# Attention on one core: a head's last two key and value pieces are split in its own first slots, and the last head's weight copies begin later

## The chip, the cores and the metric

The kernel runs on one core of one Trainium2 chip. The core has a matrix engine (PE, with its weight loads shown apart as PEld), three elementwise engines (DVE, ACT, POOL) and a queue for transfers (SP), each with an instruction stream of its own that runs in order; they meet through semaphores. The metric is the device time of one execution in microseconds (us); a kernel's time is the median of its timed runs.

## The reference, cut to what matters

One decoder block on a sequence of 2048 positions, model width 1024, eight attention heads of width 128, all in 32-bit floats. The part that the change touches is the attention:

```python
s = jnp.einsum('bhqd,bhkd->bhqk', qi, k, preferred_element_type=jnp.float32) * scale
s = s + (ci[:, :, :, None] - c[:, :, None, :])            # forget gates: c is a running sum
s = jnp.where(kpos[None, :] <= qpos[:, None], s, -jnp.inf) # causal
w = jax.nn.softmax(s, axis=-1)
return jnp.einsum('bhqk,bhkd->bhqd', w.astype(v.dtype), v)
```

Before it stand a norm, the input projection and a recurrent branch; after it the output projection `w_out`, another norm and a gated embedding. The last head's part of the attention overlaps with the preparation of `w_out`.

## The kernel before, in words

**Split operands.** Every matrix product is made of three: each 32-bit operand is split into a high part (a rounded copy) and a low part (the rest), and `mm3` (lines 63 to 70) multiplies high by high, high by low and low by high. So each operand must be split before PE can read it. `split` (line 52) makes the high part on ACT (line 54) and the low part on DVE or POOL (line 60).

**Slots.** The attention runs over 8 heads, each cut into four units g = 0 to 3 of 512 query positions; unit g sees 4(g+1) key blocks of 128. A unit's key blocks each take one slot, so a head takes 4 + 8 + 12 + 16 = 40 slots, and `t0` holds the slot in which each unit begins. In this text a *place* is a slot counted from the first slot of its head (0 to 39), and heads are counted from 0. In one slot `run_slot` writes, in this order: what is listed in `before` for that slot (mostly transfers on SP); the scores of a later unit (`score_units`: PE fills a bank `sbank`, line 1298 on DVE adds the bias, writes `pr` and takes the row's minimum `m`, line 1307 on ACT takes the exponential); the value product of three slots ago (`add_values`, PE into `obank`); the turning of this slot's probabilities (`turn_probs`: PE transposes into `tbank`, line 1342; ACT makes `th`, line 54; DVE makes `tl`, line 60); a finished unit's gate (`gate_unit`, DVE, line 1370); and then what is listed in `after` (splits, masks, chores). This is the order of each engine's own instructions and nothing else: an engine that is ahead of the others runs on until a semaphore stops it, and SP is commonly some slots ahead.

**Bringing a head in.** While head h-1 runs, the keys and values of head h are loaded in eight pieces of 128x512, p = 0 to 7: even pieces are keys (512 positions each), odd ones values. `load_piece` (lines 1184 and 1186) issues the transfer into the tile `kvf`, of which there are three; `split_piece` makes `kh` or `vh` on ACT and `kl` or `vl` on POOL. A piece's buffer is free again when POOL has made the low part, so a load can be stopped on SP by the split of the piece three before it. The tiles of two successive heads lie in two pools (`kvA`, `kvB`).

**What else uses the same engines.** Each unit's queries are loaded (`qf`, line 1216) and split into `qh` on ACT (line 1235) and `ql` on DVE (line 1237). Each unit loads a row `bias` (line 1222) and four rows `dg` (line 1228), and POOL adds the causal mask to `dg` (line 1153). A finished unit's squares go to POOL (lines 1379 and 1380) and its result is stored (line 1387). In heads 0 to 6, 64 chores are laid out one every four slots, at the places 2, 6, 10 and so on: each loads something, makes one POOL operation (`scale_l`, line 1479, or `make_t`, line 1496) and stores it (lines 1482 and 1499).

**The last head** (7) brings no further head in. Instead `load_w` (line 1253), `w_high` (ACT, line 1256) and `w_low` (POOL, line 1260) copy and split the first weights of the output projection, in the tile `wst` with three buffers, eight copies into `wa` and three into `wb`; `first_low` (DVE, line 1574) splits the first of its operands at place 16. The copies read no attention data. `open_w1` gives the weights the space of pool `kvA`, which head 6 used.

The loads and splits of a head are placed by

```python
for p_ in range(8):
    a = base + (13, 16, 26, 28, 31, 33, 36, 38)[p_]
    at(before, a - 4, lambda h=h, p_=p_: load_piece(h, p_))
    at(after, a, lambda h=h, p_=p_: split_piece(h, p_))
```

where `base` is the first slot of head h-1. Within one slot the lists keep the order in which they were filled: units' loads first, then pieces, weights, chores.

Of the kernel before, what the change touches and what calls it, by code (L numbers as in the profile page):

```python
# [20 lines left out]
KD = D // P  # L21
# [26 lines left out]
def f32(ap):  # L48
    return ap.bitcast(F32)


def split(nc, src, hi, lo, eh, el):
    if eh == "act":
        nc.scalar.activation(hi, src, AF.Copy)  # L54
    elif eh == "dve":
        nc.vector.tensor_copy(hi, src)
    else:
        nc.gpsimd.tensor_copy(hi, src)
    eng = nc.vector if el == "dve" else nc.gpsimd
    eng.tensor_tensor(out=lo, in0=src, in1=f32(hi), op=ALU.subtract)  # L60
# [13 lines left out]
def hymba_kernel(ctx: ExitStack, tc: tile.TileContext, x, xT, pT, w_p, w_v, w_o, w_ple, w_pg,  # L74
                 w_gates, vecs, rows, mgrp, out):
    nc = tc.nc
# [869 lines left out]
    for i in range(8):  # L946
        h, c = jobs.pop(0)
# [30 lines left out]
    for i in range(24):  # L978
        h, c = jobs.pop(0)
# [200 lines left out]
    def load_piece(h, n):  # L1180
        c = n // 2
        f = ap.tile([P, 4, P], F32, name="kvf", bufs=3)
        if n % 2 == 0:
            nc.sync.dma_start(out=f.rearrange("p a b -> p (a b)"), in_=kT_d[h, :, c * 512:(c + 1) * 512])
        else:
            nc.sync.dma_start(out=f, in_=v_d[h, :, c * 4:c * 4 + 4])
        pieces[h, n] = f

    def split_piece(h, n):
        if n == 0:  # L1190
            s = Ctx()
            kv = kvB if h % 2 else kvA
            s.kh = kv.tile([P, S], F32R, name="kh")
            s.kl = kv.tile([P, S], F32R, name="kl")
            s.vh, s.vl = {}, {}
            heads[h] = s
        s = heads[h]
        f = pieces.pop((h, n))
        c = n // 2
        if n % 2 == 0:  # L1200
            cs = slice(c * 512, (c + 1) * 512)
            split(nc, f.rearrange("p a b -> p (a b)"), s.kh[:, cs], s.kl[:, cs], "act", "pool")
        else:
            bs, a = slice(c % 2 * 4, c % 2 * 4 + 4), c // 2
            if c % 2 == 0:
                kv = kvB if h % 2 else kvA
                s.vh[a] = kv.tile([P, 8, P], F32R, name=f"vh{a}")
                s.vl[a] = kv.tile([P, 8, P], F32R, name=f"vl{a}")
            split(nc, f, s.vh[a][:, bs], s.vl[a][:, bs], "act", "pool")
# [41 lines left out]
    def load_w(n, k):  # L1251
        w_raw[n, k] = w1s[0].tile([P, 512], F32, name="wst", bufs=3)
        nc.sync.dma_start(out=w_raw[n, k], in_=W_SOURCE[W_ORDER[n]](k))

    def w_high(n, k):
        nc.scalar.activation(WO[n % 2][k][:, :512], w_raw[n, k], AF.Copy)

    def w_low(n, k, eng):
        w = WO[n % 2][k]
        eng.tensor_tensor(out=w[:, 512:], in0=w_raw.pop((n, k)), in1=f32(w[:, :512]), op=ALU.subtract)  # L1260
# [136 lines left out]
    before = {}  # L1397
    after = {}

    def at(d, slot, f):  # L1400
        d.setdefault(max(slot, 0), []).append(f)
# [36 lines left out]
        at(after, a, lambda p_=p_: split_piece(0, p_))  # L1438
    for h in range(1, NH):
        base = t0[4 * (h - 1)]  # L1440
        for p_ in range(8):
            a = base + (13, 16, 26, 28, 31, 33, 36, 38)[p_]
            at(before, a - 4, lambda h=h, p_=p_: load_piece(h, p_))
            at(after, a, lambda h=h, p_=p_: split_piece(h, p_))

    def open_w1():
        kvA_stack.close()
# [5 lines left out]
    w1s = []  # L1453
    last0 = t0[4 * (NH - 1)] + AHEAD + 1
    at(before, last0, open_w1)
    for a, (n, k) in zip((0, 2, 3, 5, 6, 8, 9, 11, 23, 26, 29), [(0, k) for k in range(KD)] + [(1, k) for k in range(3)]):
        a += last0
        at(before, a, lambda n=n, k=k: load_w(n, k))
        at(after, a + 4, lambda n=n, k=k: w_high(n, k))
        at(after, a + 4, lambda n=n, k=k: w_low(n, k, nc.gpsimd))  # L1460

    def scales_rows():
        b = psT.tile([P, 512], F32, name="tbank")
# [553 lines left out]
```

## Time and profile before

| | |
|---|---|
| time, median of 3 runs | 2072.45 us (2070.7 to 2072.69) |
| the profiled execution, its own time | 2074.98 us |
| its span, first to last instruction | 2073.2 us |
| granted TensorE clock | 1.000 |
| busy: PE / PEld / DVE / ACT / POOL | 2057.1 / 1742.4 / 1621.7 / 1151.5 / 697.0 us |
| first and last `th` of the attention (ACT, line 54) | 1046.7 and 1587.8 us into the span |
| key and value pieces loaded within it | 58 |

Busy time is the share in which an engine had work; on PE, matmuls overlap, so a busy PE may still be held up for less than a matmul's length. An idle time in square brackets stands in the row of the instruction that ended it, with what released that instruction. The rows themselves are shown with the prediction.

### The profile page before, as it was taken

The page shows a single profiled execution, that of the slowest core. Times are in us where ns is not written, and L with a number is a line of the kernel's source. Part 1 is how long each engine was busy: PE and PEld are TensorE (multiplying, and loading weights), DVE is VectorE, ACT ScalarE, POOL GpSimd, SP SyncE. Part 2 cuts the span into 40 slices and gives each one's busy share as a digit, 9 for nine tenths or more (in the row PEclk, how much of TensorE's full clock was granted, in tenths as well). Part 3 has the DMA queues.
Part 4 walks back from the last instruction along what each step waited for, and adds up shares of the span by engine and source line. Part 5 has one row for each costly group of instructions (what it writes and reads, how often), then busy time and mean ns, then how long its engine had stood idle before and what let it go on. Part 6 is the DMA issues. An engine that isn't in the chain of part 4 may idle for free.

```text
span 2073.2 us, 31244 instructions
## 1 busy us (share of the span) xinstructions
PE 2057.1 (99%) x10599; PEld 1742.4 (84%) x10599; DVE 1621.7 (78%) x2689; ACT 1151.5 (56%) x1855; POOL 697.0 (34%) x612
## 2 busy tenths in 40 slices
PE   9999999999999999999999999999999999999999
PEld 6988888888988898888888878888888888888887
DVE  8977997696749877986388878888885778776676
ACT  7536665344237776874167767777774344442232
POOL 4333555333013335633135665666642000000000
PEclk9999999999999999999999999999999999999999
DMA  9698898987899888779867767778653887665553
GB/s 346 215 324 296 318 348 307 375 315 282 270 283 277 276 272 293 253 258 324 253 191 236 247 209 216 237 234 241 195 173 124 291 244 231 190 216 181 171 177 117
DMA packets 254675, 518.63 MB, mean 250 GB/s; under 512 B 24866, under 2 KB 91698, under 8 KB 254515
## 3 DMA queue, kind: packets, MB, share of 16 engines
q1 hardware_dynamic: 254368, 516.59, 75.7%
q8 instruction: 83, 1.36, 0.3%
q14 instruction: 78, 0.63, 0.1%
q10 hardware_dynamic: 146, 0.05, 0.0%
HBM read 314.29 MB, written 202.25 MB: 249 GB/s over the span
## 4 chain that ended last, share of the span: by engine, by line
PE 93%; DVE 4%; DMA 1%; issue 1%; ACT 1%; POOL 0%; SPq 0%; DVEq 0%; POOLq 0%; ACTq 0%
PE bank L68 15%; PE bank L70 15%; PE bank L69 15%; PE pbank L70 7%; PE pbank L68 7%; PE pbank L69 7%; PE tbank L1342 5%; PE sbank L68 4%; PE sbank L70 3%; PE sbank L69 3%; PE obank L69 3%; PE obank L70 3%; PE obank L68 3%; PE bank L1884 1%; PE tbank L1361 1%
## 5 line engine op out<-in xcount | busy, mean ns | idle before, releaser
L68 PE MATMUL bank<-XH,op 128*128 128x512 f32 x876 | 342.8, 391 | 0.9 <-DVE u L375 0.9
L70 PE MATMUL bank<-XH,op 128*128 128x512 f32 x876 | 341.4, 390 | 0.0
L69 PE MATMUL bank<-XL,op 128*128 128x512 f32 x876 | 341.4, 390 | 0.0
L375 DVE TENSOR_TENSOR c<-bank,c 128x512 f32<-128x512 f32 x280 | 186.3, 684 | 109.5 <-PE bank L70 103.0
L60 DVE TENSOR_TENSOR tl<-tbank,th 128x512 fp32r<-128x512 f32 (+1 forms) x320 | 192.0, 606 | 78.7 <-ACT th L54 77.0
L54 ACT ACTIVATE th<-tbank 128x512 fp32r<-128x512 f32 (+1 forms) x320 | 167.4, 530 | 108.7 <-PE tbank L1342 102.3
L68 PEld LDWEIGHTS bank<-XH,op 128*128 128x128 f32 x876 | 164.6, 188 | 35.1 <-ACT op L297 1.1
L69 PEld LDWEIGHTS bank<-XL,op 128*128 128x128 f32 x876 | 164.6, 188 | 34.4 <-issue 0.5
L70 PEld LDWEIGHTS bank<-XH,op 128*128 128x128 f32 x876 | 164.5, 188 | 34.2
L1307 ACT ACTIVATE pr<-pr,m 128x1024 f32<-128x1024 f32 (+14 forms) x128 | 150.3, 1175 | 36.1 <-DVE m L1298 35.3
L1342 PE MATMUL tbank<-ident,pr 128*128 128x128 f32 x1062 | 167.4, 273 | 0.0
L152 POOL TENSOR_TENSOR rsm<-rs,mhalf 128x1 f32<-128x1 f32 x16 | 8.7, 541 | 435.0 <-DVE rs L151 435.0
L1342 PEld LDWEIGHTS tbank<-ident,pr 128*128 128x128 f32 x1062 | 130.5, 140 | 27.5 <-DVE tl L60 0.3
L68 PE MATMUL sbank<-kh,qh 128*128 128x512 f32 (+3 forms) x320 | 135.3, 423 | 3.5 <-DVE m L1298 3.0
L68 PE MATMUL obank<-th,vh 128*128 128x512 f32 (+1 forms) x320 | 123.4, 386 | 1.8 <-ACT th L54 1.8
L297 ACT ACTIVATE op<-wq 128x512 fp32r<-128x512 f32 (+1 forms) x95 | 59.5, 629 | 111.1 <-PE bank L70 82.4
L69 PE MATMUL obank<-tl,vh 128*128 128x512 f32 (+1 forms) x320 | 117.9, 369 | 0.2 <-DVE tl L60 0.2
L70 PE MATMUL obank<-th,vl 128*128 128x512 f32 (+1 forms) x320 | 116.9, 365 | 0.0
L70 PE MATMUL sbank<-kh,ql 128*128 128x512 f32 (+3 forms) x320 | 115.9, 362 | 0.0
L69 PE MATMUL sbank<-kl,qh 128*128 128x512 f32 (+3 forms) x320 | 115.3, 360 | 0.0
L69 PE MATMUL bank<-XL,wr 128*128 128x512 f32 x244 | 95.1, 390 | 0.0
L68 PE MATMUL bank<-XH,wr 128*128 128x512 f32 x244 | 95.1, 390 | 0.0
(359 smaller groups left out, 5763.8 us busy)
## 6 DMA issues: line engine op xcount, KB each, us to landing
wo_d<-op SPq DMA_DIRECT2D x140, 512.0 KB, 5.3
op<-wo_d SPq DMA_DIRECT2D x79, 512.0 KB, 6.0
wr<-wo_d SPq DMA_DIRECT2D x61, 512.0 KB, 6.2
wq<-in_w_p_dram SPq DMA_DIRECT2D x40, 512.0 KB, 6.1
wst<-wt_d SPq DMA_DIRECT2D x56, 256.0 KB, 3.5
vo_d<-op SPq DMA_DIRECT2D x27, 516.0 KB, 4.3
wst<-in_w_o_dram SPq DMA_DIRECT2D x40, 256.0 KB, 3.2
X<-xr_d SPq DMA_DIRECT2D x32, 257.5 KB, 4.0
```

Source lines behind the costliest of these rows:

```text
L54: nc.scalar.activation(hi, src, AF.Copy)
L60: eng.tensor_tensor(out=lo, in0=src, in1=f32(hi), op=ALU.subtract)
L68: nc.tensor.matmul(out, lhsT=wh, rhs=xh, start=start, stop=False)
L69: nc.tensor.matmul(out, lhsT=wh, rhs=xl, start=False, stop=False)
L70: nc.tensor.matmul(out, lhsT=wl, rhs=xh, start=False, stop=stop)
L152: nc.gpsimd.tensor_tensor(out=o, in0=t, in1=mhalf[:, :n], op=ALU.pow)
L297: nc.scalar.activation(op[:, :n], self.source(i, hf), AF.Copy)
L375: nc.vector.tensor_tensor(out=o, in0=x, in1=y, op=ALU.add)
L1307: nc.scalar.activation(pr[0][:, a:z], pr[0][:, a:z], AF.Exp, bias=m2, scale=-1.0, accum_out=u.rs[:, c:c + 1])
L1342: nc.tensor.transpose(b[:, i * P:(i + 1) * P], u.P[i][:, sb * P:(sb + 1) * P], ident)
L1361: nc.tensor.transpose(b[:, i * P:(i + 1) * P], u.r4[:, i:i + 1].broadcast_to([P, P]), ident)
L1884: nc.tensor.transpose(b[:, k * P:(k + 1) * P], u.xt[:, kk * P:(kk + 1) * P], ident)
```

## The change

Two lists of slots are changed, and nothing in what is computed.

For each head h from 1 on, the split of piece 6 (the last 512 keys) moves from place 36 of head h-1 to place 6 of head h, and that of piece 7 (the last 512 values) from place 38 to place 10. Pieces 0 to 5 are split where they were. Each load is placed 7 slots ahead of its split instead of 4, but not before the slot after the split of the piece that had the same buffer: pieces 0 to 5 at the places 6, 9, 19, 21, 24, 27 (before: 9, 12, 22, 24, 27, 29), and pieces 6 and 7 at place 39 of head h-1 and place 3 of head h (before: 32 and 34). In SP's order piece 5's load thereby comes ahead of the `bias` and `dg` loads of place 29, which it followed before.

In the last head the eight copies into `wa` are made at the places 12, 13, 14, 16, 17, 18, 20, 21 (before: 8, 10, 11, 13, 14, 16, 17, 19), and the three into `wb` stay at 31, 34, 37. Their loads are issued 3 slots ahead instead of 4.

```diff
     for h in range(1, NH):
         base = t0[4 * (h - 1)]
-        for p_ in range(8):
-            a = base + (13, 16, 26, 28, 31, 33, 36, 38)[p_]
-            at(before, a - 4, lambda h=h, p_=p_: load_piece(h, p_))
-            at(after, a, lambda h=h, p_=p_: split_piece(h, p_))
+        places_ = (13, 16, 26, 28, 31, 33, 46, 50)
+        for p_, a in enumerate(places_):
+            at(before, base + max(a - 7, places_[p_ - 3] + 1 if p_ > 2 else 0), lambda h=h, p_=p_: load_piece(h, p_))
+            at(after, base + a, lambda h=h, p_=p_: split_piece(h, p_))
...
-    for a, (n, k) in zip((0, 2, 3, 5, 6, 8, 9, 11, 23, 26, 29), [(0, k) for k in range(KD)] + [(1, k) for k in range(3)]):
+    for a, (n, k) in zip((8, 9, 10, 12, 13, 14, 16, 17, 27, 30, 33), [(0, k) for k in range(KD)] + [(1, k) for k in range(3)]):
         a += last0
-        at(before, a, lambda n=n, k=k: load_w(n, k))
-        at(after, a + 4, lambda n=n, k=k: w_high(n, k))
-        at(after, a + 4, lambda n=n, k=k: w_low(n, k, nc.gpsimd))
+        at(before, a - 3, lambda n=n, k=k: load_w(n, k))
+        at(after, a, lambda n=n, k=k: w_high(n, k))
+        at(after, a, lambda n=n, k=k: w_low(n, k, nc.gpsimd))
```

## The prediction

> **What bounds the kernel now.** I read the page first: the span, PE's busy time and the engines of the chain of work that ended last.
>
> ```profile
> span 2073.2 us, 31244 instructions
> PE 2057.1 (99%) x10599; PEld 1742.4 (84%) x10599; DVE 1621.7 (78%) x2689; ACT 1151.5 (56%) x1855; POOL 697.0 (34%) x612
> PE 93%; DVE 4%; DMA 1%; issue 1%; ACT 1%; POOL 0%; SPq 0%; DVEq 0%; POOLq 0%; ACTq 0%
> ```
>
> PE sets the time, and it idles 2073.2 - 2057.1 = 16.1 us in all. A change that takes no work from PE can win only idle time, and this one only what lies in the attention. So I next cut the attention at the starts of the heads (shown: heads 1, 2, 3, 4 and 6); columns length, then busy time (and count) of PE, PEld, DVE, ACT, POOL.
>
> ```profile
> 1112.60:1178.50 65.90, 65.43 (x393) 56.27 (x392) 56.43 (x138) 47.94 (x90) 39.29 (x42) 1.00 0.77 242
> 1178.50:1247.40 68.90, 66.05 (x394) 56.29 (x393) 56.09 (x138) 48.00 (x90) 40.75 (x43) 1.00 0.71 216
> 1247.40:1313.30 65.90, 65.41 (x393) 56.28 (x392) 56.64 (x138) 48.07 (x90) 40.09 (x43) 1.00 0.76 225
> 1313.30:1379.00 65.70, 65.21 (x393) 56.37 (x392) 56.19 (x138) 47.97 (x90) 40.51 (x43) 1.00 0.70 224
> 1445.40:1510.70 65.30, 65.21 (x394) 56.20 (x393) 55.63 (x138) 48.16 (x91) 37.88 (x42) 1.00 0.69 206
> ```
>
> Two things are to be had. Head 2 (second row) is 68.90 - 65.90 = 3.0 us longer than its neighbours. And heads 1, 3 and 4 are 0.4 to 0.6 us longer than head 6 (65.90, 65.90 and 65.70 against 65.30), with PE idle 65.90 - 65.43 = 0.47 against 0.09. Third view: who held PE up within the attention (total, times, longest).
>
> ```profile
> PE sbank L68 <- DVE m L1298: 3.0, 6, 0.8
> PE obank L68 <- ACT th L54: 1.8, 1, 1.8
> ```
>
> Fourth: the timeline at these two places. In head 2, the load of piece 5 on SP, then ACT, then PE:
>
> ```profile
> 1225.46 1.66 SPq L1186 DMA_DIRECT2D kvf<-v_d  x1
> ...
> 1236.75 0.63 ACT L54 ACTIVATE vh<-kvf 128x512 fp32r<-128x512 f32 x1 [3.45 <-DMA kvf<-v_d]
> 1237.91 0.50 PE L68 MATMUL obank<-th,vh 128*128 128x512 f32 x1 [1.81 <-ACT th L54]
> ```
>
> ACT stood 3.45 us before piece 5's split because its load had not landed, and the `th` behind it in ACT's order came late. In head 3, place 37, with head 6 below it:
>
> ```profile
> 1305.54 1.29 POOL L1496 TENSOR_TENSOR qh<-qh,qh 128x512 f32<-128x512 f32 x1
> 1306.80 1.28 POOL L60 TENSOR_TENSOR kl<-kvf,kh 128x512 fp32r<-128x512 f32 x1
> 1307.18 1.45 DVE L1237 SCALAR_TENSOR_TENSOR ql<-qf,qh 128x512 fp32r<-128x512 f32 x1
> 1309.29 0.44 PE L68 MATMUL sbank<-kh,qh 128*128 128x384 f32 x1 [0.49 <-DVE m L1298]
> ...
> 1504.11 1.29 POOL L60 TENSOR_TENSOR kl<-kvf,kh 128x512 fp32r<-128x512 f32 x1 [1.69 <-ACT kh L54]
> 1505.31 0.68 DVE L1237 SCALAR_TENSOR_TENSOR ql<-qf,qh 128x512 fp32r<-128x512 f32 x1
> ```
>
> In head 3 `ql` starts while POOL makes piece 6's `kl` and takes 1.45 us; in head 6, with `kl` nearly done, 0.68. It ends about as long after `kl` as a free `ql` lasts, so DVE waits out the POOL instruction. The 0.77 us are lost by PE, whose next bank waits for the minimum behind `ql`.
>
> **Part one: head 2's late piece.** Piece 5 comes ahead of `bias` and `dg` in SP's order, so these five transfers no longer stand before it. The load itself is not issued sooner: it waits for its buffer, that of piece 2, whose `kl` ends at 1293.10 + 1.29 = 1294.39 in head 3, and it is issued at 1294.41:
>
> ```profile
> 1287.62 0.38 SPq L1222 DMA_DIRECT2D bias<-nb_d  x1
> 1288.05 2.63 SPq L1228 DMA_DIRECT2D dg<-nb_d  x4
> 1294.41 0.32 SPq L1186 DMA_DIRECT2D kvf<-v_d  x1
> 1295.33 0.61 SPq L1216 DMA_DIRECT2D qf<-qT_d  x1
> ...
> 1293.10 1.29 POOL L60 TENSOR_TENSOR kl<-kvf,kh 128x512 fp32r<-128x512 f32 x1 [6.72 <-ACT kh L54]
> ...
> DMA to landing us min/median/max: 3.3/5.1/11.2
> ```
>
> The last row is for all loads of `kvf`. Head 2's piece 5 is issued at 1225.46 and lets ACT start at 1236.75, the maximum of 11.2; at the median it would land at 1230.6, well before ACT asks for it (1236.75 - 3.45 = 1233.3). So in the profiled execution -3.0 us, with ends 0 and -3.0. The timed runs need not have this wait: the profiled execution took 2074.98 us, 2.53 more than the median of 2072.45, and one wait for a transfer is just of that size. I count half of it against the median, -1.5.
>
> **Part two: piece 6 leaves place 36.** If POOL were then free, `ql` would take 0.68 and 0.6 us would come back in each of heads 1 to 5: -3.0 us. But POOL runs on to its next instruction, which is the chore of place 38. In head 3 that is
>
> ```profile
> 1312.90 1.29 POOL L1479 TENSOR_TENSOR kvs<-kvs,pr 128x512 f32<-128x512 f32 x1
> ...
> 1298.64 1.01 SPq L1476 DMA_DIRECT2D kvs<-yl_d  x1
> ```
>
> whose input was requested at 1298.64; all loads of `kvs` land 6.1 us later at the median, so near 1304.7, before POOL ends the chore of place 34 at 1305.54 + 1.29 = 1306.83. The chore takes the place of `kl`, lasts as long (1.29 against 1.28), and `ql` waits again. Ends -3.0 and 0; I take one head in five, -0.6, since in heads 1 and 5 this chore must wait for four transfers at once. The Trainium skill (SBUF — State Buffer, Who interferes with whom) says the same of any such pair: a DVE instruction with two SBUF inputs and a GpSimd one that reads SBUF exclude each other, and the later waits in full. The rows above agree (1.45 against 0.68); by that rule alone the sum would have 0 here instead of -0.6.
>
> **Part three: the new places 6 and 10.** Two ACT copies of 0.62 and two POOL operations of 1.29 us a head arrive there. Head 4 shows the cover:
>
> ```profile
> 1326.49 0.60 ACT L54 ACTIVATE th<-tbank 128x512 fp32r<-128x512 f32 x1 [0.43 <-PE tbank L1342]
> 1333.26 0.28 ACT L54 ACTIVATE th<-tbank 128x128 fp32r<-128x128 f32 x1 [0.71 <-PE tbank L1342]
> ...
> 1327.97 0.69 DVE L60 TENSOR_TENSOR tl<-tbank,th 128x512 fp32r<-128x512 f32 x1
> 1325.58 0.95 DVE L1370 TENSOR_TENSOR gs<-on,gs 128x512 f32<-128x512 f32 x1
> 1325.94 1.75 POOL L1479 TENSOR_TENSOR kvs<-kvs,pr 128x512 f32<-128x512 f32 x1
> ```
>
> ACT idles 0.43 us after place 6 and 0.71 after place 10, against 0.62 for a copy. The 0.2 us left over at place 7 fall on a `th` that is ready at 1326.49 + 0.60 = 1327.09 and that DVE takes up at 1327.97. DVE's only SBUF-to-SBUF operation there, `gs` at place 6, is made before ACT ends that place, so the new `kl` comes after it. I take 0; without that cover each would cost what `ql` does, 0.6 in seven heads, +4.2.
>
> **Part four: what piece 5 now holds up.** SP stops at piece 5 until POOL frees the buffer, as before, but `bias` and four `dg` now stand behind it:
>
> ```profile
> SPq L1186 <- POOL kl L60: 27.0, 13, 3.7
> ...
> 1305.50 0.55 DVE L1298 CUSTOM_DVE_ANT_0 pr<-sbank,bias 128x384 f32<-128x384 f32 x1
> 1304.76 0.62 ACT L1235 ACTIVATE qh<-qf 128x512 fp32r<-128x512 f32 x1
> ...
> DMA to landing us min/median/max: 4.4/7.5/10.4
> ...
> DMA to landing us min/median/max: 3.7/6.0/9.9
> ```
>
> The last two rows are for `dg` and for `qf`. In head 3 five transfers move from 1287.62 to 1294.8, and `qf` behind them from 1295.33 by 0.38 + 2.63 = 3.0 us to 1298.3. At its median landing it is there at 1304.3, 0.4 us before ACT reads it at 1304.76; at the longest, 1308.2, ACT waits 3.5 us, and head 2 shows the price, 3.0 us of span for 3.45 of ACT. `bias`, issued at 1294.8, is read at 1305.50, 10.7 us later; the `dg`, issued up to 1297.8, land by 1305.3 at the median, are masked by POOL and read after it, the widest last. Ends 0 and +3.0 in each of heads 1 to 6, +18; I take +1.0 in all, nearer to the median landing. Piece 6 and 7 themselves have room: their loads come after SP's stop.
>
> **Part five: the last head.** Eight copies of the same length at other places. One stays at place 16, where it meets `first_low`:
>
> ```profile
> 1541.57 1.29 POOL L1260 TENSOR_TENSOR wa<-wst,wa 128x512 fp32r<-128x512 f32 x1 [1.33 <-ACT wa L1256]
> 1541.62 2.33 DVE L1574 TENSOR_TENSOR xl<-yf,xh 128x1024 fp32r<-128x1024 f32 x1
> L1617 DVE TENSOR_TENSOR xl<-yf,xh 128x1024 fp32r<-128x1024 f32 x6 | 7.3, 1219 | 0.3 <-ACT xh L1614 0.3
> ```
>
> 2.33 against 1.22 us free, as now: 0, with ends -1.1 (the meeting ends) and +1.1 (another of that kind). The first products read `wa` at place 22, after the last copy at 21, and want only its first two tiles.
>
> **The sum.** Against the profiled execution: -3.0 - 0.6 + 0 + 1.0 + 0 = -2.6, so 2074.98 becomes 2072.4. Against the median, with half of head 2's wait: -1.5 - 0.6 + 1.0 = -1.1, so 2072.45 becomes **2071.3**.
>
> **Rivals.** (a) All idle time goes: the chore is not ready in time at any head and head 2's wait was in the timed runs too: 2072.45 - 3.0 - 3.0 = 2066.4. For it: head 6, with no chore there, has the free `ql`. Against it: the request at 1298.64. (b) Slower: `qf` is late at place 36 in heads 1 to 6, because transfers that ran while SP stood now start when it goes on. Each us that ACT waits costs 3.0/3.45 = 0.87; it decides from about 1.1 us a head, where 6 x 0.95 = 5.6 exceeds what head 2 gives by 4.1: 2076.6; at 1.5 us it is 2072.45 - 1.5 + 7.8 = 2078.8. For it: 0.4 us of room at the median. Against it: two transfers of pieces 6 and 7 leave the same stretch, and `kh` leaves ACT just after `qh`. (c) The change doesn't load sooner: piece 5 is issued at the same instant, head 2's wait stays and `ql` still waits: 2072.45.
>
> **How the numbers follow.** Single measurements of this kernel cannot tell less than 0.2%, 4.1 us, from no change: faster means under 2068.3, slower over 2076.6. The forecast with its neighbourhood has 0.50, (c) 0.14, (a) 0.19, (b) 0.17. So faster 0.19, same 0.64, slower 0.17. The range reaches to (a) below and to where (b) begins to decide above: 2066.4 to 2076.6.
>
> **What would show it.** Part one: head 2 as long as its neighbours and no ACT row that waits for `kvf`. Part two: at place 37 POOL shows L1479 or L1496 where `kl` stood, and `ql` still lasts 1.4 us in heads 3 and 4; if it lasts 0.68, (a) holds. Part three: `ql` and `gs` no longer than before at the places 6 to 15. Part four: `bias` and `dg` issued behind piece 5 and the idle time of `qh` (line 1235) before `qf`, now nearly nothing; over 1 us a head is (b). Part five: `xl` at 2.33. An idle PE behind a split at place 6 or 10 would make all of it wrong.

## The result, and the profile after

The changed kernel takes 2093.76 us, the median of 4 runs (2089.99 to 2096.68), against 2072.23 us for the kernel before on the same chip: a ratio of 1.0101, 95% interval 1.0089 to 1.0113. It is 1% slower, where 2071.3 us and "no change" were forecast, and it lies far outside the range, which ended at 2076.6. Of the rivals, (b) came true, but it had been priced at 2076.6 to 2078.8 us.

The profiled execution of the changed kernel took 2094.18 us. From its page, the span and the busy times:

```profile
span 2092.4 us, 31255 instructions
PE 2064.1 (99%) x10599; PEld 1748.4 (84%) x10599; DVE 1620.9 (77%) x2689; ACT 1150.0 (55%) x1855; POOL 700.3 (33%) x612
```

The span is 2092.4 - 2073.2 = 19.2 us longer, and two things make it up. PE idles 2092.4 - 2064.1 = 28.3 us instead of 16.1: 12.2 more. And the same 10599 matmuls keep PE busy for 2064.1 us instead of 2057.1: 7.0 more. Cut by heads (heads 0, 2, 3 and 4; columns as before the change, the third from the end is the granted clock):

```profile
1045.90:1117.20 71.30, 67.16 (x387) 56.55 (x387) 56.42 (x139) 47.73 (x93) 31.87 (x37) 0.98 0.63 190
1186.20:1255.30 69.10, 66.50 (x394) 57.40 (x393) 55.87 (x137) 47.79 (x90) 41.09 (x43) 0.98 0.72 215
1255.30:1321.60 66.30, 65.20 (x394) 56.26 (x392) 55.36 (x136) 47.82 (x90) 40.11 (x41) 1.00 0.74 219
1321.60:1394.20 72.60, 67.42 (x394) 57.42 (x393) 57.63 (x139) 47.77 (x91) 41.40 (x45) 0.98 0.73 212
```

The loss is spread over the heads, head 0 among them, which already brings head 1's pieces in. Where the clock column reads 0.98, PE's busy time is 66.5 to 67.4 us; where it reads 1.00, 65.2. The waits in the attention, first of the kernel before, then of the changed one (total us, times, longest):

```profile
ACT qh L1235 <- DMA qf<-qT_d: 0.9, 1, 0.9
```

```profile
ACT qh L1235 <- DMA qf<-qT_d: 23.0, 8, 4.0
PE sbank L68 <- DVE m L1298: 18.5, 9, 4.0
SPq L1186 <- POOL kl L60: 69.1, 12, 8.2
```

ACT's wait for the queries rose from 0.9 to 23.0 us, PE's wait for the minimum `m` from 3.0 to 18.5, and SP's stops at line 1186 from 27.0 to 69.1. That line loads all the value pieces. By their times, 50.9 of the 69.1 us stand before piece 5, 5.5 to 8.2 us in each of seven heads (before the change 13.6 of the 27.0); the rest stands before piece 1, whose buffer now waits for the late split of piece 6.

Seven of PE's nine waits, 16.6 us, stand at place 36, one in each head; the other two, 0.89 and 1.07 us, follow late loads of `gs`, a finished unit's gate. The seven are the end of a chain, and the timeline of head 4 shows its links: SP from piece 5 to `qf`, then ACT, DVE and PE at place 36.

```profile
1370.22 0.32 SPq L1186 DMA_DIRECT2D kvf<-v_d  x1
1370.58 0.43 SPq L1499 DMA_DIRECT2D wt_d<-qh  x1
1371.11 0.38 SPq L1222 DMA_DIRECT2D bias<-nb_d  x1
1371.53 1.97 SPq L1228 DMA_DIRECT2D dg<-nb_d  x4
1373.55 0.43 SPq L1476 DMA_DIRECT2D kvs<-yl_d  x1
1374.07 3.12 SPq L1387 DMA_DIRECT2D ya_d<-gs  x1
1377.24 1.64 SPq L1216 DMA_DIRECT2D qf<-qT_d  x1
...
1384.69 0.63 ACT L1235 ACTIVATE qh<-qf 128x512 fp32r<-128x512 f32 x1 [4.03 <-DMA qf<-qT_d]
1385.23 0.47 ACT L54 ACTIVATE th<-tbank 128x384 fp32r<-128x384 f32 x1
...
1385.73 0.56 DVE L60 TENSOR_TENSOR tl<-tbank,th 128x384 fp32r<-128x384 f32 x1 [3.14 <-ACT th L54]
1386.21 1.69 DVE L1237 SCALAR_TENSOR_TENSOR ql<-qf,qh 128x512 fp32r<-128x512 f32 x1
...
1388.56 0.45 PE L68 MATMUL sbank<-kh,qh 128*128 128x384 f32 x1 [3.96 <-DVE m L1298]
```

SP stands before piece 5 until POOL's `kl` of piece 2 frees the buffer, up to 8.2 us (the last row of the waits). Then everything written for the places 27 to 33 comes out in one burst, and `qf` is issued 7.0 us after piece 5, where it followed by 0.92 us in head 3 of the kernel before. It lands 7.45 us later; ACT stands 4.03 us, DVE 3.14 behind ACT's `th`, and PE 3.96 behind DVE's `m`. Head 4 is the longest of the seven: over all of them `qf` is issued 3.9 to 7.0 us after piece 5 (before the change 0.9 to 3.6), ACT gets it 6.6 to 9.7 us after that, and ACT waits 2.2 to 4.0 us.

### The profile page after: what moved, and what is told of

Same layout as the page of the kernel before. It is cut to its first block, busy times and chain, and to the rows that moved or that the text cites. A ratio compares the mean times of both kernels' runs of the same rounds, so it can differ in the third digit from the quotient of the medians.

```text
span 2092.4 us, 31255 instructions
## 1 busy us (share of the span) xinstructions
PE 2064.1 (99%) x10599; PEld 1748.4 (84%) x10599; DVE 1620.9 (77%) x2689; ACT 1150.0 (55%) x1855; POOL 700.3 (33%) x612
## 5 line engine op out<-in xcount | busy, mean ns | idle before, releaser
L68 PE MATMUL sbank<-kh,qh 128*128 128x512 f32 (+3 forms) x320 | 137.2, 429 | 19.0 <-DVE m L1298 18.5
L1153 POOL TENSOR_TENSOR dg<-dg,cmask 128x128 f32<-128x128 f32 x120 | 55.9, 475 | 130.4 <-DMA dg<-nb_d 114.9
```

What stands on the lines that cost most here:

```text
L68: nc.tensor.matmul(out, lhsT=wh, rhs=xh, start=start, stop=False)
L1153: nc.gpsimd.tensor_tensor(out=dg[:, n - P:n], in0=dg[:, n - P:n], in1=cmask, op=ALU.add)
```

## Experiments

The theory to be tested (Q): the whole loss comes from one line of the list, piece 5's load at place 27, because SP stops there with the loads of the next unit behind it. Against it stood the other parts of the change: the new places of pieces 6 and 7, the last head, and more transfers under way at once.

**The one load put back.** The changed kernel, with piece 5's load at place 29 again, behind `bias` and `dg`.

```diff
-  at(before, base + max(a - 7, places_[p_ - 3] + 1 if p_ > 2 else 0), ...load_piece(h, p_))
+  at(before, base + (29 if p_ == 5 else max(a - 7, places_[p_ - 3] + 1 if p_ > 2 else 0)), ...load_piece(h, p_))
```

> The changed kernel with one thing put back: piece 5 is loaded at place 29 again, behind bias and dg. Theory Q (SP stops at piece 5 until POOL frees its buffer, so bias, dg and the queries qf of place 31 go late, and ACT waits for qf at place 36): the waits of qh (line 1235) for qf, 23.0 us in all in the changed kernel, fall under 3 us and the time is 2066 to 2073. Theory P (the new places 6 and 10 of the splits, or the last head's copies, cost the time): it stays at 2090 to 2096.

Measured: 2069.26 us against 2071.46, ratio 0.9989, interval 0.9979 to 0.9998. The loss is gone, all of it. Its waits, and SP in one head:

```profile
ACT qh L1235 <- DMA qf<-qT_d: 0.7, 1, 0.7
SPq L1186 <- POOL kl L60: 46.0, 13, 6.9
```

```profile
1282.45 0.38 SPq L1222 DMA_DIRECT2D bias<-nb_d  x1
1282.87 1.98 SPq L1228 DMA_DIRECT2D dg<-nb_d  x4
1289.71 0.32 SPq L1186 DMA_DIRECT2D kvf<-v_d  x1
1290.26 0.32 SPq L1387 DMA_DIRECT2D ya_d<-gs  x1
1290.63 0.42 SPq L1216 DMA_DIRECT2D qf<-qT_d  x1
```

SP still stands for 46.0 us in all, 24.4 of them before piece 5 and the rest before piece 1, and `qf` follows piece 5 by 0.92 us. So SP's standing still is not what costs. What is queued behind it is.

**That load alone.** The kernel before, with nothing changed but piece 5's load, two places earlier.

```diff
-  at(before, a - 4, lambda h=h, p_=p_: load_piece(h, p_))
+  at(before, a - (6 if p_ == 5 else 4), lambda h=h, p_=p_: load_piece(h, p_))
```

> The kernel before with one thing changed: piece 5 is loaded at place 27 instead of 29. Q: this alone makes the loss, 2086 to 2096, with waits of qh for qf of 15 us or more. P: no difference, 2070 to 2074.

Measured: 2110.76 us against 2071.46, ratio 1.0187, interval 1.0172 to 1.0202. One line moved by two places costs 39 us, more than the 2086 to 2096 us that were expected and more than the whole change with its 21.5. Its waits, and ACT at place 36 of head 4:

```profile
ACT qh L1235 <- DMA qf<-qT_d: 24.1, 8, 3.9
PE sbank L68 <- DVE m L1298: 27.9, 8, 4.6
```

```profile
1391.69 0.63 ACT L1235 ACTIVATE qh<-qf 128x512 fp32r<-128x512 f32 x1 [3.46 <-DMA qf<-qT_d]
1392.97 0.63 ACT L54 ACTIVATE kh<-kvf 128x512 fp32r<-128x512 f32 x1 [0.65 <-DMA kvf<-kT_d]
1393.51 0.47 ACT L54 ACTIVATE th<-tbank 128x384 fp32r<-128x384 f32 x1
```

ACT waits for `qf` as long as in the changed kernel (24.1 against 23.0 us), but here piece 6's copy and its own late load still stand between `qh` and `th`, so `th` comes 1.82 us after `qh` starts instead of 0.54, and PE waits 27.9 instead of 18.5. By these rows the move of pieces 6 and 7 took part of the damage away. The two kernels also differ in the places of other loads, and what each did here was not separated.

**A buffer more.** The changed kernel, with a fourth buffer for the raw pieces, so that piece 5's load waits for none; its place stays 27.

```diff
-        f = ap.tile([P, 4, P], F32, name="kvf", bufs=3)
+        f = ap.tile([P, 4, P], F32, name="kvf", bufs=4)
```

> The changed kernel with four buffers for the loaded pieces instead of three, so piece 5 finds a free buffer and SP does not stop there; the order of all issues stays. Q: SP's waits for POOL kl at line 1186 (69.1 us) nearly vanish, qf lands in time, 2066 to 2073. If only the order counted and not the stop, or under P: 2085 to 2096.

Measured: 2069.49 us against 2071.46, ratio 0.9989, interval 0.998 to 0.9998; SP no longer waits for `kl` at line 1186, ACT's wait for `qf` is 1.1 us. The order on SP is that of the changed kernel, the same loads are early, and nothing is lost. The order alone does no harm; it needs a stop in it.

**The queries ahead of the stop.** The changed kernel, with the load of unit 2's queries put ahead of piece 5's; `bias` and `dg` stay behind it.

```diff
-        at(before, lo - (6 if n % 4 == 2 else 4), lambda n=n: do_load_q(n))
+        at(before, lo - (10 if n % 4 == 2 else 4), lambda n=n: do_load_q(n))
```

> The changed kernel with the query load of unit 2 moved from place 31 to place 27, ahead of piece 5; SP still stops at piece 5, and bias and dg still go late. If qf alone makes Q's loss: 2067 to 2075. If bias and dg are late as well and hold DVE: 2078 to 2090. P: 2090 to 2096.

Measured: 2073.69 us against 2071.46, ratio 1.001, interval 1.0001 to 1.002. So `qf` was some 20 us of the 24.5 us between the changed kernel and the one with the load back. The rest is left with `bias` and `dg` behind the stop. Its waits (those of 5.7 us are for the queries of the next unit, not at place 36), and POOL, then PE, in head 5:

```profile
ACT qh L1235 <- DMA qf<-qT_d: 5.7, 5, 1.5
```

```profile
1389.86 0.46 POOL L1153 TENSOR_TENSOR dg<-dg,cmask 128x128 f32<-128x128 f32 x1 [2.27 <-DMA dg<-nb_d]
...
1397.32 1.27 POOL L60 TENSOR_TENSOR kl<-kvf,kh 128x512 fp32r<-128x512 f32 x1
...
1398.64 0.39 PE L69 MATMUL sbank<-kl,qh 128*128 128x256 f32 x1 [1.85 <-POOL kl L60]
```

POOL stands before late `dg`, its masks and a finished unit's squares come late, and piece 6's `kl`, now at place 6 of the head that reads it, comes 1.85 us too late for PE. How that wait is shared between SP's stop and the rest of POOL's work was not separated.

**Pieces 6 and 7 alone.** The kernel before, with only their splits at the places 6 and 10 of their own head, and their loads four slots ahead.

```diff
-            a = base + (13, 16, 26, 28, 31, 33, 36, 38)[p_]
+            a = base + (13, 16, 26, 28, 31, 33, 46, 50)[p_]
```

> The kernel before with pieces 6 and 7 alone moved: split at the places 6 and 10 of their own head, loaded 4 slots ahead of it; pieces 0 to 5 and the last head as before. If the moved splits are free and the chore takes the POOL time that kl leaves (the prediction's parts two and three): 2069 to 2072, ql of place 37 still near 1.45 us in heads 1 to 5. If they free ql: 2066 to 2068.5. If they cost time at the new places: over 2074.

Measured: 2071.03 us against 2071.66, ratio 0.9999, interval 0.999 to 1.0008: no difference. `ql` at place 37 takes 1.40 to 1.47 us in heads 1, 3, 4 and 5, and head 2 shows piece 5 late again, with 2.3 us.

**The last head alone.** The kernel before with the copies of the last head moved, as in the change.

```diff
-    for a, (n, k) in zip((0, 2, 3, 5, 6, 8, 9, 11, 23, 26, 29), ...):
+    for a, (n, k) in zip((8, 9, 10, 12, 13, 14, 16, 17, 27, 30, 33), ...):
...
```

> The kernel before with the last head's copies alone moved. The prediction's part five: no difference, 2070 to 2073, and xl of place 16 still near 2.33 us. If the later copies hold up the products: over 2074; if they free ACT and DVE: under 2069.

Measured: 2071.72 us against 2071.66, ratio 0.9999, interval 0.999 to 1.0008: no difference. The meeting at place 16 stays as it was:

```profile
1538.37 2.32 DVE L1574 TENSOR_TENSOR xl<-yf,xh 128x1024 fp32r<-128x1024 f32 x1
```

**The chore that took the place of `kl`.** The kernel with the load back at place 29, and the POOL chores of place 38 moved to place 40, the first of the next head.

```diff
-    places = range(t0[2] + 2, last0 - 8, 4)
+    places = [a + 2 if (a - 4) % 40 == 38 else a for a in range(t0[2] + 2, last0 - 8, 4)]
```

> The kernel with piece 5 loaded at place 29 (run p5back), and the chore of place 38 moved to place 40, behind the masks, so that neither kl nor a chore is on POOL when DVE makes ql at place 37. If POOL's instruction is what lengthens ql: ql falls to 0.68 us in heads 1 to 5, PE's waits for m fall from 2.6 to under 1 us, and the time is 1.5 to 3.5 us under p5back, 2066 to 2068. If something else held PE there: as p5back, 2069 to 2070.

Measured: 2067.98 us against 2071.66, ratio 0.998, interval 0.9972 to 0.9989. Place 37 of head 3, first with the chore at place 38 (the load back at place 29), POOL and DVE:

```profile
1302.09 1.31 POOL L1479 TENSOR_TENSOR kvs<-kvs,pr 128x512 f32<-128x512 f32 x1
...
1302.48 1.47 DVE L1237 SCALAR_TENSOR_TENSOR ql<-qf,qh 128x512 fp32r<-128x512 f32 x1
```

then with the chore at place 40, the last POOL instruction before `ql` and `ql` itself:

```profile
1300.61 1.29 POOL L1496 TENSOR_TENSOR qh<-qh,qh 128x512 f32<-128x512 f32 x1
...
1302.25 0.68 DVE L1237 SCALAR_TENSOR_TENSOR ql<-qf,qh 128x512 fp32r<-128x512 f32 x1
```

The time is 1.3 us under that of the kernel with the load back, where 1.5 to 3.5 were expected, and the two intervals overlap; PE's waits for `m` fell from 2.6 to 1.9 us instead of under 1, and 1.2 of these are one wait in head 4. The meeting itself is settled: with the chore away POOL ends at 1301.90, `ql` takes 0.68 us in all seven heads, and a head without other trouble is 64.9 us instead of 65.7. The Trainium skill (SBUF — State Buffer, Who interferes with whom) states the exclusion of such a pair; 1.47 against 0.68 us, by POOL's chore alone, agrees.

**Both cures.** The changed kernel with four buffers for the pieces and the chores of place 38 at place 40.

```diff
-        f = ap.tile([P, 4, P], F32, name="kvf", bufs=3)
+        f = ap.tile([P, 4, P], F32, name="kvf", bufs=4)
...
-    places = range(t0[2] + 2, last0 - 8, 4)
+    places = [a + 2 if (a - 4) % 40 == 38 else a for a in range(t0[2] + 2, last0 - 8, 4)]
```

> The changed kernel with two edits: four buffers for the raw pieces, so that piece 5's load at place 27 waits for none, and the POOL chores of place 38 moved to place 40. Theory Q (the loss is SP's stop at piece 5, and POOL's chore is what lengthens the query conversion of place 37): both idles go, ql takes about 0.7 us, no wait of SP on POOL's key conversion at L1186, and the time is that of the run with the load back at place 29 and the chore at place 40, 2068.0 us, within 1.5. Rival, that an early load of piece 5 is worth something of its own once it can't stop the queue: below 2066. Rival, that more transfers under way at once cost by themselves: above 2070, with ACT's waits for qf over 5 us in seven heads.

Measured: 2066.41 us against 2071.57, ratio 0.9976, interval 0.9967 to 0.9985: the fastest of all, 27 us under the changed kernel. It is a little under the 2066.5 to 2069.5 us that theory Q gave and above the 2066 us under which an early load would be worth something of its own; its interval overlaps that of the kernel with the load back and the chore moved. Its heads 1, 3 and 4, and what is left in head 4:

```profile
1111.80:1176.70 64.90, 64.90 (x394) 56.30 (x393) 55.18 (x138) 47.93 (x90) 38.90 (x40) 1.00 0.72 240
1241.70:1306.60 64.90, 64.90 (x394) 56.28 (x393) 55.09 (x138) 47.99 (x90) 39.89 (x42) 1.00 0.79 223
1306.60:1373.40 66.80, 65.59 (x394) 56.34 (x393) 56.11 (x138) 48.00 (x91) 40.56 (x42) 1.00 0.79 226
```

```profile
1334.89 0.69 DVE L1370 TENSOR_TENSOR gs<-on,gs 128x512 f32<-128x512 f32 x1 [1.55 <-DMA gs<-gT_d]
1337.61 1.71 DVE L1237 SCALAR_TENSOR_TENSOR ql<-qf,qh 128x512 fp32r<-128x512 f32 x1
...
1340.05 0.50 PE L68 MATMUL sbank<-kh,qh 128*128 128x512 f32 x1 [1.16 <-DVE m L1298]
```

In the first two rows PE has no idle time at all. Head 4 lost 1.9 us to another late load, of `gs`, after which DVE met a `vl` of POOL; this was not pursued.

## Why the prediction was wrong, by its steps

**What bounds the kernel** held: PE throughout, and little idle time to be had.

**Part one** (head 2's late piece, -3.0 in the profiled execution, half against the median): the wait is gone, and the changed kernel's ACT waits for no `kvf` in the attention. It recurs: the profiles of the two kernels that keep the load's place and its neighbours, pieces 6 and 7 alone and the last head alone, show it again, with 2.3 and 2.9 us of ACT's time. But PE stood behind it only 0.7 and 1.3 us there, against 1.8, so to count half of it does not look wrong. With the load back at place 29 ACT's wait is 0.9 us although the order of piece 5, `bias` and `dg` is that of before; which of the earlier loads helps there stays open.

**Part two** (the chore takes the place of `kl`, -0.6): the mechanism is right, as the runs with `qf` in time show. With the load back, and with four buffers, `ql` at place 37 still takes 1.44 to 1.48 us in heads 1, 3, 4 and 5, and it falls to 0.68 when the chore is moved. The one head in five that was to get free does not show: with four buffers head 2 has 1.47 as well, so 0 would have been nearer than -0.6. In the changed kernel itself the sign that the prediction gave failed: `qf` is so late that the chore is often over before `ql`, which takes 0.68 in heads 1, 2, 3, 5 and 6 and 1.67 and 1.69 in heads 0 and 4, at a far greater loss. The 0.77 us that the meeting was said to cost a head show as 65.7 - 64.9 = 0.8.

**Part three** (places 6 and 10 cost 0) and **part five** (the last head, 0): right, with 0.9999 for each by itself. Without part four the sum was -1.5 - 0.6 = -2.1, and with the load back and with four buffers the medians are 2.2 and 2.0 us under the kernel before. That the size agrees so well is luck in part, since part two gave next to nothing of it.

**Part four** is the step that failed: "+1.0 in all" for what piece 5 holds up. In the profiled execution it was 19.2 + 3.0 (head 2's gain) = 22.2 us. The mechanism was named, and as rival (b) too; its size was wrong in three terms.

- *The issue.* `qf` was to slip by the two rows moved past it, 0.38 + 2.63 = 3.0 us, to 3.9 us behind piece 5. In heads 3 and 6 it did just that, 3.85 and 3.86 us; in the other five it slipped to between 4.4 and 7.0. In head 4, with 7.0, two more rows stood behind the stop, of chores (0.43 each), and the store `ya_d` took 3.12 us of SP where head 3 of the kernel before shows 0.32. All that SP would have spread over its stop of 8 us it now issues in a row.
- *The landing.* It took longer than the median 6.0 us in all seven heads, 6.6 to 9.7 us, and 8.8 and 9.4 in heads 3 and 6, where the issue was as forecast. Issue and landing together are 12.6 to 14.5 us instead of 9.9. In head 4 `qf` is there 14.47 us after piece 5 (1370.22 to 1384.69), so 4.6 late against a room of 0.4: 4.2, and ACT's row shows 4.03. The forecast took the room from medians.
- *The price.* Rival (b) took 0.87 us of span per us that ACT waits. The 23.0 - 0.9 = 22.1 us of waits stand against 22.2, 1.0 each. 14.6 of these are idle time, 12.2 net and 2.4 that covered head 2's gain. The other 7.6, 7.0 and head 2's 0.6, are longer busy time of PE, which no part of the prediction had; five stretches at half clock after the longer idle times can account for it, at 8.5 us at most. The division is rough: kernels at full clock throughout differ by up to 3.4 us in PE's busy time (2057.1 before the change, 2053.7 with the load back and the chore moved), and 2.0 us of PE's waits came from `gs`.

Even the upper end of part four, +18 in the sum, was exceeded. The value was put next to the median landing, because `qf` still had 0.4 us of room there; but 0.4 us beside a slip of 3.0 was no cover, and the chance of 0.17 for (b) was too small. Rival (b) also counted heads 1 to 6, where head 0 is struck as well. (In its sum 6 x 0.95 is 5.7, not 5.6, which changes its price by 0.1 us.)

## What to carry to other kernels

A load that waits for a buffer stops every load behind it on its queue; before moving one ahead, list what it is moved past and when each of these is read, and count the whole burst that comes out after the stop, not only the rows that are moved. A buffer more takes the stop away and makes the order harmless. When an engine's operation is waiting out another's instruction, look at what comes next in that other engine's order: here it was the chore behind it that had to be moved.

## What the runs showed of the hardware that was not expected

**The matrix clock halves after less than 2 us of idle time.** The changed kernel in stretches, behind head 4's idle 3.96 us, then with two shorter idle times, 1.91 and 1.74 us (columns: length, busy time and count of PE, PEld, DVE, ACT, POOL, granted clock):

```profile
1390.00:1392.00 2.00, 2.00 (x7) 1.51 (x6) 1.19 (x6) 1.47 (x4) 0.57 (x2) 0.50 0.48 118
1394.00:1396.00 2.00, 2.00 (x15) 1.87 (x15) 1.20 (x4) 1.73 (x3) 0.30 (x1) 1.00 0.90 282
...
1454.20:1457.60 3.40, 1.49 (x9) 0.93 (x7) 1.91 (x5) 2.09 (x5) 2.31 (x3) 1.00 1.05 372
1457.60:1461.10 3.50, 3.50 (x11) 2.81 (x10) 2.29 (x10) 2.25 (x5) 0.29 (x1) 0.51 0.75 243
1461.10:1464.50 3.40, 3.40 (x22) 3.09 (x22) 2.43 (x6) 1.68 (x4) 0.92 (x2) 1.00 0.79 188
...
1522.40:1525.90 3.50, 1.76 (x10) 1.09 (x8) 1.77 (x4) 2.09 (x5) 0.97 (x1) 1.00 0.77 204
1525.90:1529.40 3.50, 3.50 (x19) 3.03 (x20) 2.80 (x10) 1.96 (x4) 0.92 (x2) 1.00 0.52 183
```

At 0.50, PE makes 7 matmuls in 2 us instead of 15. In the changed kernel the half clock came five times and lasted 3.41 us each time. Its starts, at 1112.91, 1181.18, 1249.45, 1389.39 and 1457.66 us, lie 20, 20, 41 and 20 times 3.413 us apart, so the clock seems to be set anew on a grid of that step. In the step just before each start PE idled 2.04, 2.19, 2.11, 2.58 and 1.91 us; after 1.74 us in one step the half clock did not come. Where the queries went ahead, it came after 1.85 us. The 1.81 us of head 2 in the kernel before, after which it did not come, are no counterexample, as they lie across two steps of that run's grid, 1.04 and 0.77 us. So the idle time in one step that halves the clock lies here between 1.74 and 1.85 us.

Five times 3.41 us at half speed are 8.5 us at most, and PE's busy time rose by 7.0. The Trainium skill (TensorE: Matmul & The Clock Gate, Part 1) has the same 3.41-us free-running window and half clock, but asks for a whole window of idle time; these rows had it with little over half of one. With piece 5's load moved alone, five of its seven half-clock stretches lasted 6.83 us, two steps; in these PE idled 1.06 us or more in the first of the two. The lost clock there is 2070.3 - 2057.1 = 13.2 us of PE's busy time.

**A queue's own issue can lengthen.** Most of SP's rows for one transfer in the attention last 0.3 to 0.6 us. Behind piece 5's stop in the changed kernel each of the seven heads has one of 2.0 to 3.1 us: 3.12 us in head 4, and in six of the heads it is the ninth transfer that SP issues from the end of the stop on, all within 4.5 us. The kernel before has such rows too, of up to 2.33 us (`kvs` at 1106.00, `gs` at 1267.12), so they come without such a stop too. What makes them long was not tested.
